# Difference operands kept in SBUF instead of streamed, with small tables fetched per stage

## The chip, the cores and the metric

The kernel runs on one core of a Trainium2 chip. The metric is the device time of one execution in microseconds (us). Three runs of the kernel before took 2766.94, 2767.81 and 2770.83 us; the median is 2767.81 us. A profile is one further execution, recorded by the hardware profiler. TensorE is called PE (its weight loads PEld), VectorE DVE, ScalarE ACT, GpSimd POOL and SyncE SP. SP and POOL are used here mainly to issue transfers, each from its own queue.

## The reference

A two-layer encoder works on 256 rows of 4096 numbers in float32. Cut to what matters:

```python
for l in range(DEPTH):                      # DEPTH = 2
    h = rmsnorm(x, norm_w[l])
    proj = h @ w_in[l]                      # 4096 -> 11264
    aq, ak, av, ag, rq, rk, rv, rg = jnp.split(proj, SPLIT_POINTS, axis=-1)
    aq = apply_axial_rope(rmsnorm(aq, q_norm[l]), rope) * attn_scale    # 16 heads
    ak = apply_axial_rope(rmsnorm(ak, k_norm[l]), rope)                 # 4 heads
    a_out = silu(ag) * gqa_attention(aq, ak, av)
    rq, rk = apply_axial_rope(rq, rope), apply_axial_rope(rk, rope) * ret_scale   # 8 heads
    r = bidirectional_retention(rq, rk, rv, log_gf, log_gb)             # decay by distance
    r_out = silu(rg) * rmsnorm(r, ret_norm[l])
    x = x + jnp.concatenate([a_out, r_out], axis=-1) @ w_out[l]         # 4096 -> 4096
return rmsnorm(x, final_norm)
```

Nearly all the arithmetic is in the two matrix products of each layer. The tables of cosines and sines, the distances between rows and the four norm weights are small.

## The kernel before, in words

**Products.** Every float32 product is made of three matmuls (`product`, lines 723 to 725): both factors are split into a high and a low part, and high times high, high times low and low times high are summed in PSUM. The operand, 256 rows of 4096 inputs, is kept in SBUF as 16 pairs of 256 inputs. The weights come from DRAM in pages of 128x1024 numbers (512 KB). A block computes two groups of 512 output columns from all 16 pairs. It saves multiplications with Strassen-like sums: the four pairs in `SEVEN` use seven products on sums of operand and weight quarters, the twelve others (`EIGHTS`) use eight products, two of which take a difference of the operand's two row halves. There are 11 blocks of the input projection and 4 of the output projection in a layer, 30 blocks in all, each with 372 matmuls of 512 columns. With 672 matmuls of 256 columns for attention and retention that makes 11832.

**Operand arrays.** `split_pair` makes a pair's arrays: `x7h`, `x7l` for the four, `x8h`, `x8l` for the twelve, and for each of the twelve also a difference array `x3` of 256 KB. The difference arrays do not stay in SBUF. They are stored to `x3_dram` (line 522, from a buffer called `xg`, or from the buffer of the first use where `direct` is set), and each block loads each of them again (`third`, line 1034) into one of `THIRDS` = 4 buffers. A load has to wait until PE has done with the pair that held the buffer before. In the profile the tile is called `x` and the DRAM array `x_dram`; `x2_dram`, the residual, has the same name there.

**Weights.** SP issues the page loads (line 366, tile `wraw`, 5 buffers). ACT rounds a page to its high part (`whi`), DVE subtracts to get the low part (`wlo`), and the buffer is then free for the next load. For the pairs in `SEVEN` DVE also makes sums of pages (`wsum`). One page in each group of four pairs is `far`: ACT makes its high part and the negative of it, and POOL issues a transfer that adds the page from DRAM to that (`flo`, line 391). That instruction is put in POOL's queue together with the two ACT instructions that it waits for.

**Order of the work.** The program is unrolled, and a planner that runs at build time sets the order on each engine: `Now` is its time, `ve` and `ac` add estimated durations of DVE and ACT work, and `LANDING` = 9 us is its estimate for a transfer. After each product `tick` puts in what there is time for: low parts, splits of the next operand, and steps of `tasks` (rotary, attention, retention and so on, of which only the first in the list is stepped) and `lanes`. `room` decides if there is time before the next weight page is due. Engines execute their instructions in that order, each waiting only for the semaphores it needs. If an estimate is too short, the waiting instruction holds up all that stands behind it on its engine.

**Pages.** Work arrays of 512 KB share `PAGES` = 10 buffers, counted in `held`. A new block takes two of them when its product M1 is done (`follow`, `combine`). If too many are held, or two heavy tasks are open, `follow` puts it off, and at the first of the last four products it runs tasks until there is room, whatever PE has to wait.

**Retention.** `retention_keys` stores rotated keys and queries to DRAM. `retention_weights` loads them for two heads (`rk`, `rq`, lines 886 and 887, from POOL), makes the decay array `D` out of the distances in `cst`, and multiplies by the scores that PE puts in the PSUM tile `ps`. `retention_pair` then multiplies by the values, norms, gates, transposes and puts the result away as operand for the output projection. The last two chunks of an operand (pairs 12 to 15) are not stored but split directly, late, during the first block that uses them.

**Small data.** The tables (`cst`, 512 KB), both layers' query and key norm weights (`qn`, `kn`) are loaded once by SP in `load_small` and stay in SBUF. A retention or final norm weight is loaded into a buffer `gain` of its own when it is needed.

Of the kernel before, what the change touches and what calls it, by code (L numbers as in the profile page):

```python
# [35 lines left out]
PAGES = 10  # L36
# [17 lines left out]

THIRDS = 4
# [150 lines left out]
def hybrid_encoder(  # L206
# [27 lines left out]
    x3_dram = tc.dram_tile([2, NP, P, 2, 2, P], F32R, name="x3_dram")  # L234
# [22 lines left out]
    cst = t(cp, [P, C_END], "cst")  # L257
    nw = t(cp, [P, DEPTH * KT], "nw")
    qn = t(cp, [P, DEPTH * HD], "qn")
    kn = t(cp, [P, DEPTH * HD], "kn")  # L260
# [9 lines left out]
    def load_small():  # L270
        nc.sync.dma_start(cst, consts)
        nc.sync.dma_start(dec, decay.partition_broadcast(P))
        nc.sync.dma_start(qn, q_norm.partition_broadcast(P))
        nc.sync.dma_start(kn, k_norm.partition_broadcast(P))

    def log_sigmoid():

        n = DEPTH * 2 * RET_HEADS
        u, s, s2, p, a = (t(cp, [P, n], f"ls{i}") for i in range(5))
# [13 lines left out]
        ve.tensor_scalar_mul(lgn, p, -2.0)  # L293

# [4 lines left out]
    def rope_tables(kind, l):  # L299

        cm = cst[:, C_COS:C_SIN].rearrange("p (m d) -> p m d", m=MT)
        sm = cst[:, C_SIN:C_D].rearrange("p (m d) -> p m d", m=MT)
# [4 lines left out]
        g = (kn if kind == "ak" else qn)[:, l * HD : (l + 1) * HD]  # L307
# [18 lines left out]
    class Weights:  # L326


        def __init__(self):
# [27 lines left out]
            self.raw, self.later = [], []  # L357
# [27 lines left out]
        def far_parts(self, g, src):  # L385

            g.hi = t(wp, [P, 2, NB], "fhi", FAR, F32R)
            g.lo = t(wp, [P, 2, NB], "flo", FAR, F32R)
            ac.copy(g.hi, src)
            ac.activation(g.lo, f32(g.hi), AF.Copy, scale=-1.0)  # L390
            nc.gpsimd.dma_start(g.lo, g.src[0], accum_op=ALU.add)  # L391
            g.high_at, g.low_at = ac.until, ac.until + FAR_LANDING
            self.load()

        def begin(self, g):
# [6 lines left out]
            elif g.kind == PAGE_A:  # L402
                self.a, self.b = self.raw.pop(0), self.raw.pop(0)
# [3 lines left out]
            elif g.kind == PAGE_T:  # L407
                self.u = t(wp, [P, 2, NB], "wsum", 2)
# [8 lines left out]

        def low_parts(self, all=False):
# [3 lines left out]
        def take(self):  # L422
            g = self.pages[self.at]
            self.at += 1
            while g.low_at is None:
                self.later.pop(0)[1]()
            return g

# [27 lines left out]
    stored_at = [0.0, 0.0]  # L456
    version = [0] * NP
    late, waiting, stored = [], [], set()

    def split_pair(p, v, l=None, direct=False):  # L460
# [22 lines left out]
        if p in SEVEN:  # L483
            hi = t(ap, [P, 7, P], "x7h", len(SEVEN), F32R)
# [14 lines left out]
            ve.tensor_sub(lo[:, 2:7, :], f, f32(hi)[:, 2:7, :])  # L499
        else:  # L500
            hi = t(ap, [P, 2, SEQ], "x8h", NP - len(SEVEN), F32R)
            lo = t(ap, [P, 2, SEQ], "x8l", NP - len(SEVEN), F32R)
            high(hi, v)
# [4 lines left out]
            if direct:  # L508
                while live[0] == THIRDS:
                    yield  # L510
                live[0] += 1
            else:
                while not stored_at:
                    yield
                free = stored_at.pop(0)
                if now.t < free:
                    yield free - now.t
            g = t(ap, [P, 2, 2, P], "x3" if direct else "xg", THIRDS if direct else 2, F32R)
# [3 lines left out]
            nc.gpsimd.dma_start(x3_dram[version[p] % 2, p], g)  # L522
            if direct:
                thirds[p] = g
            else:
                stored_at.append(ve.until + LANDING)
# [3 lines left out]
        operand[p] = (hi, lo)  # L530
# [3 lines left out]
    def split_operand(c, l=None, rest=0.0, direct=False):  # L534
        v, full[c] = full[c], None
        for k in range(2):
            p = 2 * c + k
            waiting.append(Lane(split_pair(p, v[:, 2 * k : 2 * k + 2, :], l, direct)))
            waiting[-1].pair, waiting[-1].ready = p, now.t + rest

    def split_late():
        split_operand(*late.pop(0), direct=True)
# [34 lines left out]
    class Turn:  # L577
# [19 lines left out]
        def step(self, forced=False):  # L597
# [6 lines left out]
            if c < self.fetched and self.freed > 2 * c + 1 and (forced or len(waiting) < SPLITS):  # L604
                split_operand(c, self.l, self.at[c] - now.t, self.first is not None)
# [28 lines left out]
    class Lane:  # L634
        def __init__(self, steps, heavy=True):
            self.heavy = heavy
            self.steps, self.ready, self.last, self.done, self.value = steps, 0.0, 0.0, False, None

        def step(self):
# [9 lines left out]
            if ac.until > a:  # L649
                self.last = max(self.last, ac.until)  # L650
            if rest == "PE":
# [8 lines left out]
    def clear():  # L660
        while tasks and tasks[0].done:
            tasks.pop(0)
        lanes[:] = [v for v in lanes if not v.done]

    def advance():

        clear()
        one = min(lanes + tasks[:1], key=lambda v: v.ready)
# [4 lines left out]
    def tick():  # L673

        weights.low_parts()
        while turning and turning[0].step():
            pass
        while True:
# [3 lines left out]
            for v in waiting[:SPLITS] + (lanes + tasks[:1] if room else []):  # L682
# [65 lines left out]
    def rotary(v, L, kind):  # L748
# [3 lines left out]
        C, S = L.tables.get(kind) or rope_tables(kind, L.index)  # L752
# [40 lines left out]
    def gate(acc, L, gain=None):  # L793
# [12 lines left out]
        if gain is not None:  # L806
            ve.tensor_mul(acc, acc, gain.unsqueeze(1).to_broadcast([P, MT, NB]))
        yield
# [73 lines left out]
    def retention_weights(L, i):  # L882
# [4 lines left out]
        nc.gpsimd.dma_start(qT, rq_dram[i])  # L887
        landed = max(now.t, L.stored) + LANDING
        D = page([P, 4, SEQ], "D")
        for e in range(2):  # L890
# [4 lines left out]
            ve.tensor_scalar_mul(v, cst[:, C_D:C_END], lf)  # L895
            ve.scalar_tensor_tensor(v, cst[:, C_D:C_END], lb, v, op0=ALU.mult, op1=ALU.min)
            yield
        ac.activation(D, D, AF.Exp)
# [53 lines left out]
    def retention_pair(L, i, gacc, vacc):  # L952
        gain = t(sp, [P, NB], "gain", 1)
# [7 lines left out]
        drop(4)  # L961
        mixT = gacc.rearrange("p m (a s) -> p (m a) s", a=2)
# [3 lines left out]
    def keys_values(L, kacc, vacc):  # L966
# [9 lines left out]
        L.tables = {}  # L976
        kT = yield from rotary(kacc, L, "ak")
# [410 lines left out]
```

## Time and profile before

| what | value |
|---|---|
| runs | 2766.94, 2767.81, 2770.83 us; median 2767.81 |
| profiled execution: time, span of its instructions | 2769.11 us, 2767.4 us |
| granted TensorE clock, mean | 0.987 |
| PE busy | 2646.9 us (96%) |
| DVE, ACT, POOL busy | 2067.6 (75%), 2024.1 (73%), 433.9 us (16%) |
| moved by transfers | 743.22 MB, mean 269 GB/s |
| SP's queue (q1), POOL's queue (q0), of the 16 engines' time | 54.1%, 31.2% |

A busy PE is not a PE that is never late: matmuls overlap, and a row lasts longer than the distance to the next one. What matters is that distance. In a stretch where nothing is late it is 0.227 us for 512 columns and 0.118 us for 256. The lines of the waits view give, for an engine and a line, who ended the idle time before it, in us in total, in times, and the longest. In the view by windows each row has the length of a stretch, then for each engine its busy time with the number of instructions, then the granted clock, the share of time in which the transfer engines were busy, and GB/s.

### The profile page before, as it was taken

The numbers are of one execution on the slowest core, as the hardware profiler recorded it, in microseconds if no ns is written. First come the engines' busy times: TensorE is split into PE (matmuls) and PEld (weight loads), VectorE is DVE, ScalarE is ACT, GpSimd is POOL, SyncE is SP. The second block draws the span as 40 slices with busy tenths as digits, with TensorE's granted clock in tenths as the row PEclk, the third lists the DMA queues.
The fourth block names the chain that finished last, engine by engine and source line by source line (L and its number), as shares of the span: only waits on it lengthen the run. The fifth ranks groups of instructions, "written<-read, shape, count | busy, mean of one in ns | idle before, by whom it ended". The sixth has DMA issues, their size and how long they took to land.

```text
span 2767.4 us, 35090 instructions
## 1 busy us (share of the span) xinstructions
PE 2646.9 (96%) x11832; PEld 2188.1 (79%) x11832; DVE 2067.6 (75%) x2489; ACT 2024.1 (73%) x3176; POOL 433.9 (16%) x665
## 2 busy tenths in 40 slices
PE   7999999999989999999899999999999899999997
PEld 5787788778878878888678877887888788788886
DVE  8786777778767887666678777777787588876665
ACT  6778888887657767666877688888876576775554
POOL 0121111111111121111121111111111112211110
PEclk9999999999999999999999999999999999999999
DMA  8997778778878998999898978887788799989996
GB/s 279 313 296 233 241 243 276 235 227 282 281 231 270 309 296 257 298 294 299 290 288 274 277 230 257 247 253 242 237 273 272 231 287 309 298 253 276 279 284 226
DMA packets 244724, 743.22 MB, mean 269 GB/s; under 512 B 26688, under 2 KB 33600, under 8 KB 244544
## 3 DMA queue, kind: packets, MB, share of 16 engines
q1 hardware_dynamic: 148048, 522.04, 54.1%
q0 software_dynamic: 96496, 218.93, 31.2%
q8 instruction: 94, 1.54, 0.2%
q14 instruction: 86, 0.70, 0.1%
HBM read 697.88 MB, written 42.99 MB: 268 GB/s over the span
## 4 chain that ended last, share of the span: by engine, by line
PE 68%; DMA 10%; DVE 9%; ACT 8%; issue 5%; POOL 1%; SPq 0%; DVEq 0%; ACTq 0%; POOLq 0%
PE M L724 22%; PE M L723 22%; PE M L725 22%; DMA wraw<-in_w_in 7%; DVE wlo L191 5%; ACT whi L191 2%; DMA rq<-rq_dram 2%; ACT pr L191 2%; PE ps L723 1%; PE ps L725 1%; PE ps L724 1%; ACT ca L191 1%; ACT rot L191 1%; DVE wsum L191 1%; ACT fhi L191 1%
## 5 line engine op out<-in xcount | busy, mean ns | idle before, releaser
L191 ACT CAST whi<-wraw 128x1024 fp32r<-128x1024 f32 x842 | 815.9, 988 | 463.8 <-PE M L725 283.1
L191 DVE TENSOR_TENSOR wlo<-wraw,whi 128x1024 fp32r<-128x1024 f32 x842 | 943.9, 1143 | 214.0 <-ACT whi L191 208.4
L724 PE MATMUL M<-wlo,x8h 128*128 128x512 f32 x1806 | 708.4, 392 | 5.6 <-DVE wlo L191 5.5
L723 PE MATMUL M<-whi,x8h 128*128 128x512 f32 x1806 | 707.8, 392 | 4.5 <-ACT whi L191 4.5
L725 PE MATMUL M<-whi,x8l 128*128 128x512 f32 x1806 | 706.3, 391 | 0.0
L724 PEld LDWEIGHTS M<-wlo,x8h 128*128 128x128 f32 x1806 | 341.8, 189 | 77.8 <-DVE wlo L191 8.2
L723 PEld LDWEIGHTS M<-whi,x8h 128*128 128x128 f32 x1806 | 342.0, 189 | 75.4 <-ACT whi L191 4.9
L725 PEld LDWEIGHTS M<-whi,x8l 128*128 128x128 f32 x1806 | 341.8, 189 | 71.6
L191 DVE TENSOR_TENSOR wlo<-wsum,whi 128x1024 fp32r<-128x1024 f32 x240 | 292.7, 1220 | 86.0 <-ACT whi L191 85.5
L724 PE MATMUL M<-wlo,x7h 128*128 128x512 f32 x840 | 329.3, 392 | 13.5 <-DVE wlo L191 13.5
L725 PE MATMUL M<-whi,x7l 128*128 128x512 f32 x840 | 328.1, 391 | 6.5 <-DVE x7l L191 6.5
L723 PE MATMUL M<-whi,x7h 128*128 128x512 f32 x840 | 328.4, 391 | 4.2 <-DVE cb L191 4.1
L1034 POOL DMA_DIRECT2D x<-x_dram x339 | 227.7, 717 | 663.7 <-PE M L725 636.7
L191 ACT CAST whi<-wsum 128x1024 fp32r<-128x1024 f32 x240 | 251.8, 1049 | 97.4 <-PE M L725 92.9
L191 DVE TENSOR_TENSOR wsum<-wraw 128x1024 f32<-128x1024 f32 x120 | 146.7, 1222 | 192.9 <-DMA wraw<-in_w_in 111.7
L724 PE MATMUL M<-wlo,x 128*128 128x512 f32 x602 | 236.7, 393 | 14.8 <-DVE wlo L191 14.8
L723 PE MATMUL M<-whi,x 128*128 128x512 f32 x602 | 236.0, 392 | 11.6 <-ACT whi L191 11.6
L725 PE MATMUL M<-whi,x 128*128 128x512 f32 x602 | 235.5, 391 | 0.0
L391 POOL DMA_DIRECT2D flo<-in_w_in x86 | 76.1, 885 | 855.6 <-ACT flo L191 788.2
L724 PEld LDWEIGHTS M<-wlo,x7h 128*128 128x128 f32 x840 | 158.4, 189 | 49.6 <-DVE wlo L191 17.8
L725 PEld LDWEIGHTS M<-whi,x7l 128*128 128x128 f32 x840 | 158.5, 189 | 39.9 <-DVE x7l L191 7.2
L723 PEld LDWEIGHTS M<-whi,x7h 128*128 128x128 f32 x840 | 158.4, 189 | 38.2 <-DVE cb L191 4.9
(222 smaller groups left out, 3511.8 us busy)
## 6 DMA issues: line engine op xcount, KB each, us to landing
wraw<-in_w_in SPq DMA_DIRECT2D x703, 512.0 KB, 5.1
wraw<-in_w_out SPq DMA_DIRECT2D x256, 512.0 KB, 5.8
x<-x_dram POOLq DMA_DIRECT2D x339, 256.0 KB, 7.4
flo<-in_w_in POOLq DMA_DIRECT2D x86, 512.0 KB, 7.5
flo<-in_w_out POOLq DMA_DIRECT2D x32, 512.0 KB, 7.7
full<-next_dram POOLq DMA_DIRECT2D x18, 512.0 KB, 9.7
next_dram<-ca POOLq DMA_DIRECT2D x15, 512.0 KB, 7.6
x_dram<-xg POOLq DMA_DIRECT2D x27, 256.0 KB, 6.0
```

The lines of the kernel that those rows point to most:

```text
L191: return call(out, *args, **kwargs)
L391: nc.gpsimd.dma_start(g.lo, g.src[0], accum_op=ALU.add)
L723: nc.tensor.matmul(out, a[0], b[0], start=start, stop=False)
L724: nc.tensor.matmul(out, a[0], b[1], start=False, stop=False)
L725: nc.tensor.matmul(out, a[1], b[0], start=False, stop=stop)
L1034: nc.gpsimd.dma_start(thirds[p], x3_dram[(phase - 1) % 2, p])
```

## The change

`x3_dram`, `third` and `THIRDS` go. Each of the twelve difference arrays has a buffer of its own in SBUF, is written once for each operand by `split_pair`, and is read there by every block. The split no longer waits for a free buffer or a finished store. To make room, `cst`, `qn`, `kn`, the buffer `gain` and the arrays of `log_sigmoid` go, and there are 9 pages instead of 10. A stage fetches what it needs into a shared page: `plain_tables` loads cosines and sines, and for attention the two norm weights, when `keys_values` or `retention_keys` begins; `retention_weights` loads the distances as `dist`; a norm weight takes a page as well.

Three rules of the planner change too. The transfer that completes a far page is put into POOL's queue when ACT's part is planned to be done (`adds`), and not with it. Only one pair of `SEVEN` at a time is in the middle of its split (`sums_of`), and low parts of an older sum of pages are put in before a new sum is made (`sums_low`). A retention pair that has only its transpose left counts as `tail`: the next retention weights may then be stepped beside it, and it no longer holds off the next block.

```diff
-PAGES = 10
+PAGES = 9
-THIRDS = 4
...
-    cst = t(cp, [P, C_END], "cst")
-    qn = t(cp, [P, DEPTH * HD], "qn")
-    kn = t(cp, [P, DEPTH * HD], "kn")
...
+    def plain_tables(l=None):
+        v = page([P, 3, SEQ], "tables")
+        nc.sync.dma_start(v[:, :2, :], consts[:, C_COS:C_D].rearrange("p (a b) -> p a b", a=2))
+        if l is not None:
+            for i, g in enumerate((k_norm, q_norm)):
+                nc.sync.dma_start(
+                    v[:, 2, i * HD : (i + 1) * HD], g[l * HD : (l + 1) * HD].partition_broadcast(P)
+                )
+        return v
...
-            nc.gpsimd.dma_start(g.lo, g.src[0], accum_op=ALU.add)
             g.high_at, g.low_at = ac.until, ac.until + FAR_LANDING
+            self.adds.append((ac.until, partial(nc.gpsimd.dma_start, g.lo, g.src[0], accum_op=ALU.add)))
...
+        def add(self, now_all=False):
+            while self.adds and (now_all or self.adds[0][0] <= now.t + 0.5):
+                self.adds.pop(0)[1]()
...
+            g = t(ap, [P, 2, 2, P], "x3", NP - len(SEVEN), F32R)
             high(hi, v)
             yield
             low(lo, v, hi)
             ve.tensor_sub(x0, x0, x1)
             yield
-            if direct:
-                while live[0] == THIRDS:
-                    yield
-                live[0] += 1
-            else:
-                while not stored_at:
-                    yield
-                free = stored_at.pop(0)
-                if now.t < free:
-                    yield free - now.t
-            g = t(ap, [P, 2, 2, P], "x3" if direct else "xg", THIRDS if direct else 2, F32R)
             high(g[:, 0], x0)
             yield
             low(g[:, 1], x0, g[:, 0])
-            nc.gpsimd.dma_start(x3_dram[version[p] % 2, p], g)
-            if direct:
-                thirds[p] = g
-            else:
-                stored_at.append(ve.until + LANDING)
...
+    def running():
+        return tasks[: 2 if len(tasks) > 1 and tasks[0].tail and not tasks[1].heavy else 1]
...
         nc.gpsimd.dma_start(qT, rq_dram[i])
+        dist = page([P, 2 * SEQ], "dist")
+        nc.sync.dma_start(dist, consts[:, C_D:C_END])
+        yield LANDING
...
-            ve.tensor_scalar_mul(v, cst[:, C_D:C_END], lf)
-            ve.scalar_tensor_tensor(v, cst[:, C_D:C_END], lb, v, op0=ALU.mult, op1=ALU.min)
+            ve.tensor_scalar_mul(v, dist, lf)
+            ve.scalar_tensor_tensor(v, dist, lb, v, op0=ALU.mult, op1=ALU.min)
...
-        gain = t(sp, [P, NB], "gain", 1)
+        gain = page([P, NB], "gain")
...
+        yield "tail"
         mixT = gacc.rearrange("p m (a s) -> p (m a) s", a=2)
...
         L.tables = {}
+        L.plain = plain_tables(L.index)
         kT = yield from rotary(kacc, L, "ak")
...
     def retention_keys(L, r, kacc, qacc):
+        L.plain = plain_tables()
+        yield LANDING
...
-            if finished[0][0] == "M1" and (held[0] > PAGES - 2 or sum(v.heavy for v in tasks) > 1):
+            if finished[0][0] == "M1" and (held[0] > PAGES - 2 or sum(v.heavy and not v.tail for v in tasks) > 1):
...
-    def third(p, phase):
-        need(p, phase)
-        if p in thirds:
-            return
-        live[0] += 1
-        thirds[p] = t(ap, [P, 2, 2, P], "x3", THIRDS, F32R)
-        nc.gpsimd.dma_start(thirds[p], x3_dram[(phase - 1) % 2, p])
...
-                a = [x3[p][:, i, index[0], :] for i in range(2)]
+                a = [operand[p][2][:, i, index[0], :] for i in range(2)]
```

## The prediction

> **What bounds the kernel now.** I read the page first, then the stretches by window, then who PE waited for, then single stalls in the timeline. The page and the view of transfers give the engines, the two queues and the traffic that the change removes:
>
> ```profile
> span 2767.4 us, 35090 instructions
> PE 2646.9 (96%) x11832; PEld 2188.1 (79%) x11832; DVE 2067.6 (75%) x2489; ACT 2024.1 (73%) x3176; POOL 433.9 (16%) x665
> ...
> q1 hardware_dynamic: 148048, 522.04, 54.1%
> q0 software_dynamic: 96496, 218.93, 31.2%
> ...
> x<-x_dram POOLq DMA_DIRECT2D x339, 256.0 KB, 7.4
> ...
> x_dram<-xg POOLq DMA_DIRECT2D x27, 256.0 KB, 6.0
> x_dram<-x POOLq DMA_DIRECT2D x21, 256.0 KB, 5.6
> ```
>
> PE is the bound, but not by 96%. In fed stretches the timeline starts a 512-column matmul every 0.2268 us (49.07, 49.30) and a 256-column one every 0.118 (797.66, 797.78). 11160 x 0.2268 + 672 x 0.118 = 2610 us that no schedule here takes away. PE starts at 9.7 us, its last matmul at 2750.7; what follows, 16.6 us, is the end. The rest, 2767.4 - 9.7 - 2610.2 - 16.6 = 131 us, is lost on the way. The window view shows where; each line is a length, then PE's busy time:
>
> ```profile
> 389.00:477.00 88.00, 88.00 (x407) 73.54 (x406) 68.80 (x77) 76.52 (x133) 14.88 (x22) 1.00 0.86 268
> 755.00:856.00 101.00, 91.27 (x412) 75.92 (x411) 66.81 (x74) 64.19 (x94) 14.42 (x22) 0.95 0.76 232
> 940.00:1038.00 98.00, 92.38 (x423) 76.82 (x422) 85.96 (x125) 68.13 (x105) 21.90 (x36) 0.98 0.92 299
> 1287.00:1386.00 99.00, 89.88 (x377) 72.06 (x377) 68.75 (x100) 71.97 (x126) 20.97 (x34) 0.95 0.90 288
> 1386.00:1480.00 94.00, 88.25 (x371) 71.40 (x370) 72.89 (x103) 69.62 (x113) 16.10 (x25) 0.96 0.91 280
> ```
>
> A quiet block loses nothing, even with transfers busy 86% of the time. The others lose 6 to 12 us, partly at a lower granted clock. I split the trace by blocks of 372 large matmuls and took each one's length less its 0.2268 and 0.118 steps. The first block loses 17.9, attention blocks (2 to 6 and 17 to 21) 44.3, block 1 1.8, retention blocks (7 to 10, 22 to 25) 43, and blocks 14 and 15, where layer 1 begins, 24.0. PE's waits name the causes:
>
> ```profile
> PE M L724 <- DVE wlo L191: 33.9, 21, 3.0
> PE ps L723 <- DMA rq<-rq_dram: 29.2, 4, 9.7
> PE M L723 <- ACT whi L191: 16.1, 4, 9.7
> PE M L725 <- DVE x7l L191: 6.5, 2, 5.0
> ```
>
> The last fence shows two kinds of them, one at 777 to 792 us, one at 339 to 353: POOL's issues, PE's stall, and what DVE waited for.
>
> ```profile
> 777.80 0.88 POOL L887 DMA_DIRECT2D rq<-rq_dram  x1
> 792.29 0.58 PE L723 MATMUL ps<-rq,rk 128*128 128x256 f32 x1 [9.73 <-DMA rq<-rq_dram]
> 339.24 0.88 POOL L391 DMA_DIRECT2D flo<-in_w_in  x1 [11.61 <-ACT flo L191]
> 339.80 0.88 POOL L1034 DMA_DIRECT2D x<-x_dram  x1
> 341.60 0.54 POOL L1034 DMA_DIRECT2D x<-x_dram  x1 [0.92 <-PE M L725]
> 349.76 0.53 POOL L1034 DMA_DIRECT2D x<-x_dram  x1 [7.62 <-PE M L725]
> 352.58 1.23 DVE L191 TENSOR_TENSOR wsum<-wraw 128x1024 f32<-128x1024 f32 x1 [4.17 <-DMA wraw<-in_w_in]
> ```
>
> **The change part by part.** Of the built programs I take only order: a distance between two instructions is counted in the matmuls between them, at 0.2268 us. Arithmetic is untouched: PE, DVE and ACT have the same instructions. POOL issues 244 transfers instead of 631 (339 loads and 48 stores of 256 KB less, 101 MB of 743); SP issues 1036 instead of 1021.
>
> *Retention loads, -36 us.* Before, the scores stand 13 and 26 large matmuls (2.9 and 5.9 us) behind the issue of `rq` in the second and fourth retention pair of a layer: the planner was forced, since a new block could not begin while two heavy tasks were open. Such a load lands in 6.7 to 14.4 us, so PE stood 9.9, 5.4, 9.3 and 5.2 us, and restarted at half speed. Blocks 8, 10, 23 and 25 lose 38.2 us in all. Afterwards, through `tail`, the scores stand 76 to 91 matmuls (17 to 21 us) behind it. I leave 2 us. The delay of retention by 80 to 150 matmuls that buys this lies under weight products; it costs at the end of each layer (below).
>
> *Retention scores, -4.* The waits of 2.4 and 2.0 us in blocks 7 and 22 (loss 4.9) sit behind a page that took 10.7 us. The two scores move from 15 to 48 matmuls apart.
>
> *Late weight pages in attention, -15; at 107 us, -2.* Nine DVE stalls end with a page (as at 352.58), and PE waits 18.0 us behind them, some 20 with slow restarts. POOL's queue explains them: `flo` holds it until ACT is done, then `flo` and two or three `x` loads go out together. At 344.9 to 352.5 us 2.75 MB were in flight, 0.75 of it `x`. If landing follows the bytes, 7.6 us becomes 5.5, more than the 1.6 us that PE waited. The same sum leaves 1.8 of 3.2 at 213 us, 0.7 of 2.3 at 332, and nothing to 0.8 at the others: 4.5 stay. At 107 us 0.75 of 4.75 MB go: 1.7 off. If landing did not depend on `x`, this item is 0; if every such stall goes, -22.
>
> A different split is thinkable. The Trainium skill, DMA: Bandwidth & Descriptors, section Queues, rings and completion order, states that each transfer engine takes turns between queues, a packet of each. By that, a page is slowed as long as POOL's queue holds anything at all, and `flo`, `kv` and stores stay there; bursts would only end sooner, and this item and the next would be nearer the small end. The trace of before cannot tell: every late page of attention had `x` beside it.
>
> *Start of layer 1, -14.* Blocks 14 and 15 lose 24.0 us. At 1296 us 6.25 MB are in flight, 0.75 of it `x`; `ca<-in_x` takes 15.5 us where the planner counts 9. POOL stood 11.3 us for a store, with other stores behind it. In the new order the residual's stores come up to 75 matmuls (17 us) earlier and the last splits up to 28 (6 us). I take a little over half; bounds -6 and -22, since the chain of store, load and split remains.
>
> *The burst at 114 us, -2.* Block 1 loses 1.75 us behind the steps of `log_sigmoid`; they now stand apart.
>
> *Tables for the keys, +5.* New, and with no time given to land: in block 1 the table products stand 10 matmuls (2.3 us) behind SP's issue of the key norm, with a low part behind them that PE needs 13 matmuls after that issue. The nearest transfer is `gain`, 3.7 to 12.5, median 4.6 us; `kn` took 8.9. With 4.6, DVE goes on 20 matmuls after the issue, spends 0.95 us on the tables (143.25 to 144.20) and 1.2 on the low part: PE waits 3.7 us, and about 1 more at half speed. Ends: 2.8 at 3.7 and 8.0 at 8.9; I take the median, being of the same size and form. In layer 1 the next low part has 5 us of slack: 0 at 4.6, 3.3 at 8.9. I take 0.5.
>
> *Distances, +1; norm weights, 0.* Eight `dist` loads (256 KB) have 7.0 to 8.2 us before DVE reads them; 3 of 14 `gain` loads took over 9. Bounds 0 and +8. `gain` has 6.1 to 10.4 us, before 5.2 to 9.1, and nobody waited for it then. The rotary tables have 9.1 to 10.7.
>
> *Late splits, +3.* Pairs 14 and 15 of each mixer output come later: the array that PE first needs is written 3 matmuls before its use, against 40 before. I put 1.5 us each, between 0 and the 5.2 us of the other late operand (45.81 us). Nine pages instead of ten cause no forced work elsewhere in the order.
>
> *Unchanged:* the start to 47 us (the same order, 15.4 us lost, DVE full), four stalls in each layer's attention behind ACT's queue (`room` waiting for `pr`), 17 us in all, the 16.6 us at the end. `flo` has 13.9 us or more until its use, and lands in 7.6 (11.7 at most).
>
> Sum: -36 - 4 - 15 - 2 - 14 - 2 + 5 + 0.5 + 1 + 3 = -63.5. The profiled execution took 2769.1 us, 1.3 above the median, so it stands for the runs; 2767.8 - 63.5 = **2704** us.
>
> **The rivals.**
>
> *Small relief.* Pages land no sooner. For it: a stretch at 96% transfer share (1480 to 1565 us) loses nothing, one at 76% (198 to 295) does, so share is not what counts, and `flo` and `kv` remain in the bursts. Then only the order helps: -36 - 1 - 6 - 2, and +7 and +3 for tables, +2 for distances, +3 for late splits: -30, 2738 us. Against it: every late page of attention had `x` beside it.
>
> *Larger relief.* Shorter bursts also clear the start of layer 1 and all late pages: -38 - 5 - 22 - 2 - 22 - 2 + 3 + 1 = -87, 2681 us. Against it: the chain from residual to split has transfers of its own.
>
> *Slower: SP's fetches hold DVE.* DVE runs in order, and a table that is late holds low parts that PE needs. 22 fetches a run are exposed. They have 2.3 to 10.7 us, 8.2 on average; to eat 63.5 us they must be 2.9 us late on average, so land in 11.1. At 11.5 us the time would be 22 x 3.3 - 63.5 = +9, 2777 us. Against it: 1 of 14 `gain` loads took that long.
>
> *The arrays are fetched all the same.* Excluded: no load of `x3` is left in the order.
>
> **How the numbers follow.** Forecast 0.62, small relief 0.19, larger relief 0.08, slower 0.09, within 0.2% (5.5 us, about what a measurement here can tell) 0.02. The range, 2676 to 2742, leaves out slower and part of the small relief. Faster 0.89.
>
> **What would show it.** `x<-x_dram` gone from the transfer lines, 640 MB instead of 743; no PE wait for `rq`; in PE's waits `wlo` from 34 to about 20; a PE stall of 3 to 6 us near 120 to 150 us behind a DVE wait for `tables`; a page's median landing from 5.4 to below 5; blocks 14 and 15 at 10 us lost. I am wrong if DVE or PE waits for `dist`, `tables` or `gain` add up to tens of us, if SP's queue waits on a page buffer, or if late pages wait as long as now.

## The result, and the profile after

The changed kernel takes 2701.78 us (median of four runs, 2699.30 to 2705.79), the kernel before 2767.38 us in the same comparison: a ratio of 0.9769, 95% interval 0.9744 to 0.9793. The profiled execution took 2701.46 us with a span of 2699.7 us. PE's first matmul starts at 11.1 us, the last at 2682.9; with the same 2610 us of steps, 61.7 us are lost on the way, against 130.9 before.

The page of the changed kernel gives the span and the engines (busy time, share, number of instructions):

```profile
span 2699.7 us, 34139 instructions
...
PE 2633.3 (98%) x11832; PEld 2182.0 (81%) x11832; DVE 2068.9 (77%) x2489; ACT 2025.1 (75%) x3176; POOL 218.1 (8%) x278
```

Its view of transfers gives the traffic, the two queues, and for a kind of transfer the number, the size and the median time to landing:

```profile
DMA packets 191149, 644.82 MB, mean 239 GB/s; under 512 B 20736, under 2 KB 27904, under 8 KB 190976
...
q1 hardware_dynamic: 150208, 525.19, 56.4%
q0 software_dynamic: 40768, 117.46, 19.9%
...
wraw<-in_w_in SPq DMA_DIRECT2D x703, 512.0 KB, 4.5
wraw<-in_w_out SPq DMA_DIRECT2D x256, 512.0 KB, 4.8
```

The difference arrays are gone from POOL's queue (218.93 MB there before), DVE and ACT do what they did, and a weight page lands sooner (medians 5.1 and 5.8 us before). The view by windows, cut at the blocks that answer to the five shown of before (4, 8, 10, 14, 15), gives for each stretch the length, PE's busy time, and near the end the granted clock and the share of transfer time:

```profile
386.00:475.00 89.00, 89.00 (x411) 74.35 (x411) 69.44 (x78) 77.50 (x135) 6.97 (x8) 1.00 0.76 232
745.00:837.00 92.00, 92.00 (x438) 77.38 (x438) 73.66 (x86) 63.95 (x93) 8.85 (x11) 1.00 0.76 233
921.00:1011.00 90.00, 89.03 (x411) 74.09 (x409) 82.17 (x117) 62.97 (x90) 13.68 (x20) 1.00 0.87 283
1269.00:1359.00 90.00, 86.14 (x371) 70.13 (x370) 70.96 (x104) 73.23 (x129) 10.41 (x14) 0.98 0.83 270
1359.00:1445.00 86.00, 85.51 (x377) 70.16 (x376) 71.27 (x99) 67.92 (x111) 7.80 (x9) 1.00 0.84 252
```

The blocks of the two retention stretches had lost 11.9 and 7.7 us at a clock of 0.95 and 0.98; now they lose 0.2 and 1.3 us and the clock is 1.00. The start of layer 1 shrinks from 99 and 94 us to 90 and 86. PE's waits name what is left (us in total, times, longest):

```profile
PE M L735 <- DVE wlo L189: 26.7, 15, 5.0
PE M L734 <- ACT whi L189: 11.6, 2, 11.1
PE M L736 <- DVE x7l L189: 6.0, 2, 5.0
```

No line for `rq` remains; 29.2 us stood there before. What is new stands in block 1, where the timeline shows DVE's last work before the tables, SP's fetch of the key norm, DVE's first use of the tables with the idle time before it, the low part behind it, and PE:

```profile
137.02 1.82 DVE L189 TENSOR_TENSOR wlo<-wraw,whi 128x512 fp32r<-128x512 f32 x2
...
140.16 0.66 SPq L298 DMA_DIRECT2D tables<-in_k_norm  x1
...
146.39 0.29 DVE L189 TENSOR_TENSOR C<-tables 128x128 f32<-128x128 f32 x1 [7.55 <-DMA tables<-in_k_norm]
147.34 1.22 DVE L189 TENSOR_TENSOR wlo<-wsum,whi 128x1024 fp32r<-128x1024 f32 x1
148.61 0.79 PE L735 MATMUL M<-wlo,x7h 128*128 128x512 f32 x1 [5.05 <-DVE wlo L189]
```

So the time is near the forecast of 2704 us, and the blocks that gained are those that it named. The question for the experiments is whether they gained for the reasons given.

### The profile page after: what moved, and what is told of

Its sections match the earlier page's. It is cut to its first block, busy times and chain, and to the rows that moved or that the text cites. A ratio compares the mean times of both kernels' runs of the same rounds, so it can differ in the third digit from the quotient of the medians.

```text
span 2699.7 us, 34139 instructions
## 1 busy us (share of the span) xinstructions
PE 2633.3 (98%) x11832; PEld 2182.0 (81%) x11832; DVE 2068.9 (77%) x2489; ACT 2025.1 (75%) x3176; POOL 218.1 (8%) x278
## 4 chain that ended last, share of the span: by engine, by line
PE 79%; DVE 7%; ACT 5%; issue 4%; DMA 4%; SPq 0%; POOL 0%; DVEq 0%; POOLq 0%; ACTq 0%
PE M L735 26%; PE M L734 25%; PE M L736 25%; DVE wlo L189 4%; DMA wraw<-in_w_in 3%; ACT pr L189 2%; ACT whi L189 2%; DMA wraw<-in_w_out 1%; PE ps L736 1%; PE ps L734 1%; PE ps L735 1%; DVE ca L189 0%; DVE cb L189 0%; DVE wsum L189 0%; ACT fhi L189 0%
## 5 line engine op out<-in xcount | busy, mean ns | idle before, releaser
L189 ACT CAST fhi<-wraw 128x1024 fp32r<-128x1024 f32 x118 | 124.2, 1052 | 73.6 <-PE M L736 64.8
```

What stands on the lines that cost most here:

```text
L189: return call(out, *args, **kwargs)
```

## The experiments

The table holds every kernel: the median time, the ratio to before with its interval, and PE's loss in groups of blocks in the profiled run (the length of a block less its 0.2268 and 0.118 steps, as in the prediction). *Attention* is blocks 2 to 6 and 17 to 21, *retention* 8, 10, 23 and 25.

| kernel | us | ratio | block 1 | attention | retention | 11, 26 | 14, 15 |
|---|---|---|---|---|---|---|---|
| before | 2767.4 | 1 | 1.8 | 44.3 | 38.2 | 0.1 | 24.0 |
| changed | 2701.8 | 0.9769 (0.9744 to 0.9793) | 7.2 | 28.3 | 2.6 | 0.3 | 7.4 |
| changed, no `tail` | 2736.8 | 0.9906 (0.9883 to 0.9930) | 7.7 | 26.7 | 2.9 | 34.9 | 7.4 |
| before + `tail` | 2733.4 | 0.9874 (0.9850 to 0.9899) | 1.0 | 46.2 | 5.3 | 0.1 | 21.3 |
| before + wait | 2744.3 | 0.9916 (0.9894 to 0.9938) | 0.5 | 47.0 | 7.8 | 4.3 | 22.2 |
| before + `adds` | 2725.3 | 0.9864 (0.9837 to 0.9891) | 1.9 | 36.7 | 7.4 | 0.1 | 16.9 |
| changed, streamed | 2743.9 | 0.9924 (0.9896 to 0.9952) | 10.8 | 45.3 | 6.0 | 11.9 | 21.6 |
| changed, half streamed | 2718.2 | 0.9821 (0.9798 to 0.9844) | 7.4 | 32.5 | 3.6 | 6.7 | 13.4 |
| changed, `adds` undone | 2706.4 | 0.9790 (0.9763 to 0.9818) | 7.3 | 27.2 | 2.5 | 0.3 | 14.4 |
| changed, tables early | 2691.6 | 0.9743 (0.9722 to 0.9764) | 0.0 | 28.9 | 2.5 | 0.2 | 7.1 |
| and softmax put off | 2677.4 | 0.9678 (0.9658 to 0.9698) | 0.0 | 9.8 | 3.8 | 0.3 | 6.8 |

Block 0 and the start of the first matmul (8.4 to 11.1 us) scatter by a few us between runs of all kernels and are left out.

### Is it `tail` that keeps rq ahead of its scores?

The prediction's largest term, the retention loads, rests on `tail`. The first kernel takes it out of the changed one.

```diff
         drop(4)
-        yield "tail"
         mixT = gacc.rearrange("p m (a s) -> p (m a) s", a=2)
```

> The changed kernel without the rule that a retention pair with only its transpose left counts as tail; all else is as changed. Theory A (the prediction's step on the retention loads): tail is what keeps rq ahead of its scores, so PE's waits for rq come back (some 25 to 30 us, four of them, in the second and fourth pair of a layer) and the time is 30 to 36 us above the changed kernel, 2732 to 2738 us. Theory B: the loads are early because the new wait for the distances stands ahead of the moment from which the landing of rq is counted (about 18 us of allowance, 9 before) and because POOL's queue is shorter; tail only lets the end of a layer's retention keep up. In the order of this kernel the scores stand 79, 84, 78 and 111 large matmuls behind the issue of rq, which speaks for B. Then no wait for rq above 1 us; the loss comes in blocks 11 and 26, where the split of pairs 14 and 15 is late, by about 13 us in each: about 2728 us. The times are near each other; the row of rq and the loss of blocks 8, 10, 11, 23, 25 and 26 tell the two apart.

It took 2736.8 us: inside theory A's interval by its time. The rows say the opposite. These are PE's waits in the kernel without `tail`, the longest three, and no line for `rq` follows:

```profile
PE M L734 <- ACT x L189: 29.1, 2, 14.6
PE M L735 <- DVE wlo L189: 26.9, 13, 5.1
PE M L734 <- ACT whi L189: 11.1, 2, 10.3
```

The retention blocks lose 2.9 us as in the changed kernel. The loss stands in blocks 11 and 26, 17 us each, where PE waits 14.6 us for a split of pair 14 or 15 (`x` is the difference array of such a pair) and restarts at half speed. In the changed kernel `rq` does not need `tail`; what `tail` does there is to let a layer's retention end in time for the late splits. Theory B holds, with its price sized at 13 instead of 17 us a layer.

Then what makes `rq` late before? Each of the three rules that touch it was put alone into the kernel before. First `tail`:

```diff
+        return tasks[: 2 if len(tasks) > 1 and tasks[0].tail and not tasks[1].heavy else 1]
...
+        yield "tail"
...
-            if finished[0][0] == "M1" and (held[0] > PAGES - 2 or sum(v.heavy for v in tasks) > 1):
+            if finished[0][0] == "M1" and (held[0] > PAGES - 2 or sum(v.heavy and not v.tail for v in tasks) > 1):
```

> The kernel before with the tail rule alone (a retention pair with only its transpose left lets the next retention weights step beside it and no longer holds off a block). The difference arrays are streamed, the distances stay in SBUF, and no wait is added. In the built order the scores stand 73, 62, 87 and 42 large matmuls behind the issue of rq (before: 73, 13, 87, 26), that is 16.6, 14.1, 19.7 and 9.5 us; such a load landed in 6.7 to 14.4 us before. If tail alone is enough (the prediction's mechanism), PE's waits for rq shrink from 29.2 us to under 3 and blocks 8, 10, 23 and 25 lose under 10 us instead of 38: 2730 to 2738 us. If the load is late because of POOL's queue and slow landing whatever tail does, rq waits of 10 us or more stay: 2745 us or more.

The time is 2733.4 us, and of 29.2 us this is left in PE's waits:

```profile
PE ps L728 <- DMA rq<-rq_dram: 1.6, 2, 0.8
```

So `tail` alone is enough where nothing else is changed, though it isn't needed where the rest is. Next the wait that the change adds for the distances, in the kernel before, where the distances don't need it:

```diff
         nc.gpsimd.dma_start(qT, rq_dram[i])
+        yield LANDING
         landed = max(now.t, L.stored) + LANDING
```

> The kernel before with one line more: the wait of LANDING (9 us of planned time) that the change puts into retention_weights, behind the issue of rk and rq and ahead of the moment from which their landing is counted. No tail, difference arrays streamed, distances in SBUF. In the built order the scores stand 79, 58, 93 and 94 matmuls behind the issue of rq: 17.9, 13.2, 21.1 and 21.3 us. If the allowance alone is enough (theory B), PE's waits for rq go from 29.2 us to under 3; the retention of a layer ends later without tail, so that blocks 11 and 26 may lose up to 10 us each in late splits (17 each in the changed kernel without tail): 2733 to 2753 us. If only tail or the shorter queue cures it, rq waits of 10 us or more stay and the time is 2755 us or more.

2744.3 us. No wait for `rq` is left among PE's waits; the retention blocks lose 7.8 instead of 38.2 us and blocks 11 and 26 lose 4.3. The added 9 us of allowance are enough too. What both work around is seen in POOL's timeline of the kernel before, ahead of the issue of `rq` at 777.80 us that the prediction shows:

```profile
763.82 0.54 POOL L1034 DMA_DIRECT2D x<-x_dram  x1 [9.44 <-PE M L725]
775.65 0.88 POOL L391 DMA_DIRECT2D flo<-in_w_in  x1 [11.30 <-ACT flo L191]
776.22 0.87 POOL L1034 DMA_DIRECT2D x<-x_dram  x1
776.75 0.88 POOL L572 DMA_DIRECT2D next_dram<-ca  x1
777.27 0.88 POOL L886 DMA_DIRECT2D rk<-rk_dram  x1
...
1006.20 0.54 POOL L522 DMA_DIRECT2D x_dram<-xg  x1 [7.01 <-issue]
1009.08 0.88 POOL L391 DMA_DIRECT2D flo<-in_w_in  x1 [2.34 <-ACT flo L191]
```

In the second pair POOL stands 11.3 us at the transfer that completes a far page, until ACT is done with it. Four more transfers stand behind it, `rq` the last of them, and go out within 2.2 us: `rk` lands in 12.4, `rq` in 14.4 us. In the fourth pair (the last two lines) POOL is idle 7.0 us before the store of a difference array and 2.3 us before a far page; `rq` goes out at 1010.76 us and lands in 11.0. Layer 1 repeats both, at 2150.78 and 2382.65 us.

The planner had left its 9 us for `rq`. Its own order, as it comes out when the kernel before is built, has 42 large matmuls (9.5 us) between the issue and the scores in both pairs, and no block was put off until it had to force a step. In the built program, which lists the engines' queues together, 13 and 26 are left, since POOL's queue is behind there too. With `tail` alone the planner still leaves 42 in the second pair, and the built program has 62: the issue stands elsewhere in POOL's queue, where POOL waits 5.3 us at the far page ahead of it. The third rule of the change, `adds`, is aimed at the far page, and the prediction gave it no term. It changes nothing that the planner counts, and yet moves the built distances to 33 and 37. Alone in the kernel before:

```diff
-            nc.gpsimd.dma_start(g.lo, g.src[0], accum_op=ALU.add)
             g.high_at, g.low_at = ac.until, ac.until + FAR_LANDING
+            self.adds.append((ac.until, partial(nc.gpsimd.dma_start, g.lo, g.src[0], accum_op=ALU.add)))
...
+            if g.far:
+                self.add(True)
...
+        weights.add()
```

> The kernel before with one rule of the change alone: the transfer that completes a far page is put into POOL's queue when ACT's part is planned to be done, and not with it. In the profile of before POOL stands 11.3 us at such a transfer until 775.65 us, with the store of an operand and the loads of rk and rq behind it; then five transfers go out within 2.2 us. In the built order of this kernel the scores stand 73, 33, 91 and 37 large matmuls behind the issue of rq (before: 73, 13, 87, 26), so 7.5 and 8.4 us in the second and fourth pair instead of 2.9 and 5.9. If POOL's blocked queue is what makes rq late, about half of PE's 29.2 us for rq goes (4.6 and 2.5 us less in each layer, 14 us in all, more if the transfers no longer go out in one burst): 10 to 16 us stay and blocks 8, 10, 23 and 25 lose 18 to 26 us instead of 38: about 2745 to 2755 us. If the lateness has nothing to do with that queue, the waits stay above 24 us and the time within 5 us of 2765.

It gave more than was expected: 2725.3 us, below the 2745 to 2755, with 4.6 us of waits for `rq`. The waits of this kernel, PE's for `rq`, then POOL's for PE at a load of a difference array and for ACT at a far page:

```profile
PE ps L730 <- DMA rq<-rq_dram: 4.6, 2, 2.9
...
POOL x L1041 <- PE M L732: 1300.4, 218, 13.3
POOL flo L433 <- ACT flo L191: 330.5, 93, 18.0
```

POOL's two lines of before:

```profile
POOL flo L391 <- ACT flo L191: 1081.5, 102, 18.0
POOL x L1034 <- PE M L725: 636.7, 114, 18.5
```

POOL waits hardly less in all: what it no longer waits at far pages it waits at the loads of `x`, whose buffer PE still holds. What changed is what stands behind the waiting instruction. In the second pair of layer 0 `rq` lands in 10.7 instead of 14.4 us; the median landing of `x` falls from 7.4 to 5.9 us, that of `rq` from 9.4 to 7.5. The faster landing is why the waits for `rq` shrink by more than the shift in order. Attention and the start of layer 1 gain too (7.6 and 7.1 us). A weight page's median is no better than before there (5.3 and 5.8 us), but DVE's waits for pages before a sum fall from 192.8 to 150.6 us; that fewer bursts make the worst pages less late is the likely reason, and not shown page by page. One rule of a few lines, with the arrays still streamed, gives 1.4% of the whole change's 2.3%.

### Do the bytes of the difference arrays make pages late?

The changed kernel with the arrays streamed again, and everything else kept:

```diff
-            g = t(ap, [P, 2, 2, P], "x3", NP - len(SEVEN), F32R)
+            g = t(ap, [P, 2, 2, P], "x3" if direct else "xg", THIRDS if direct else 2, F32R)
...
+            nc.gpsimd.dma_start(x3_dram[version[p] % 2, p], g)
...
+        nc.gpsimd.dma_start(thirds[p], x3_dram[(phase - 1) % 2, p])
```

> The changed kernel with the difference arrays streamed from DRAM again (48 stores and 339 loads of 256 KB on POOL's queue); the shared pages, the tables per stage, tail, the put-off transfer of far pages and the rules for sums stay. If the traffic and its place in POOL's queue made the gains in attention and at the start of layer 1 (the prediction: 15 and 14 us, measured 16 and 17), blocks 2 to 6 and 17 to 21 lose 40 us or more instead of 28, blocks 14 and 15 lose 20 or more instead of 7, a page's median landing goes back from 4.6 to about 5.4 us, and the time is 2725 to 2745 us. If the new order and the put-off far transfers made them, these blocks stay within 4 us and the time is at most 2708 us. PE's waits for rq: the scores stand 76 to 86 matmuls behind the issue here too, so both expect none.

2743.9 us, as the traffic theory had it. Attention loses 45.3 us again and the start of layer 1 21.6. The landing of a page goes back, and past the 5.1 and 5.8 us of before, in the view of transfers of this kernel:

```profile
wraw<-in_w_in SPq DMA_DIRECT2D x703, 512.0 KB, 5.4
wraw<-in_w_out SPq DMA_DIRECT2D x256, 512.0 KB, 6.2
x<-x_dram POOLq DMA_DIRECT2D x339, 256.0 KB, 5.9
```

Retention stays cured (waits for `rq` of 0.8 us). Something not expected came in blocks 11 and 26, 11.9 us. Two of the four waits in this line, 3.5 us each, stand there; why DVE's sums (`cb`) are late at that place was not followed further:

```profile
PE M L753 <- DVE cb L191: 11.1, 4, 3.5
```

Streaming brings bytes, but also 387 more instructions in POOL's queue, many of which wait for PE or DVE. To part the two, the low half of each array was streamed and the high half kept: the same transfers at the same places, of half the size. Against the streamed kernel:

```diff
-            g = t(ap, [P, 2, 2, P], "x3" if direct else "xg", THIRDS if direct else 2, F32R)
-            high(g[:, 0], x0)
+            gh = t(ap, [P, 2, P], "x3h", NP - len(SEVEN), F32R)
+            g = t(ap, [P, 2, P], "x3" if direct else "xg", THIRDS if direct else 2, F32R)
+            high(gh, x0)
             yield
-            low(g[:, 1], x0, g[:, 0])
+            low(g, x0, gh)
```

> The changed kernel with the difference arrays streamed again, but by halves: the high part of each stays in SBUF, the low part is stored and loaded. The number of transfers, their place in POOL's queue and the waits of that queue are those of the fully streamed kernel (2743.9 us); the bytes are half (387 transfers of 128 KB). If the bytes in flight make pages late, the loss that streaming brought in attention (45.3 us against 28.2), blocks 14 and 15 (21.6 against 7.4) and 11 and 26 (11.9 against 0.3) falls by about half, the median landing of a page lies between 4.6 and 5.4 us, and the time is 2716 to 2728 us. If the number of transfers and the waits in POOL's queue make them late, the time stays within 6 us of 2744.

2718.2 us: of the 42.1 us that full streaming costs, 16.4 remain at half the bytes, and a page lands in between.

```profile
wraw<-in_w_in SPq DMA_DIRECT2D x703, 512.0 KB, 4.8
wraw<-in_w_out SPq DMA_DIRECT2D x256, 512.0 KB, 5.7
x<-x_dram POOLq DMA_DIRECT2D x339, 128.0 KB, 5.1
```

So most of the loss goes with the bytes: had the number of transfers or the waits of the queue made it, the time would have stayed near 2744 us. What share those have in the 16.4 us that remain is not told apart. The groups don't halve alike: attention keeps 4.2 of 17.1 us, the start of layer 1 6.0 of 14.2, blocks 11 and 26 6.4 of 11.5. A page that lands before it is needed costs nothing, which would explain why in all the first half of the bytes was worth more than the second.

The rule `adds`, worth so much before, was then taken out of the changed kernel.

```diff
-            self.adds.append((ac.until, partial(nc.gpsimd.dma_start, g.lo, g.src[0], accum_op=ALU.add)))
+            nc.gpsimd.dma_start(g.lo, g.src[0], accum_op=ALU.add)
```

> The changed kernel, with the transfer that completes a far page put into POOL's queue at once with ACT's two instructions, as before the change. POOL then stands until ACT is done with the page, with whatever was issued later behind it. If the queue was blocked mostly to the harm of the loads of the difference arrays, which are gone, this is worth little: within 4 us of the changed kernel, 2698 to 2706 us. If the blocked queue itself was what made rq, kv and the pages late, waits for rq or late pages come back: 10 to 25 us more, 2712 to 2727 us.

2706.4 us, 4.6 more than the changed kernel's median and so just past the 4 us that were expected at most, with intervals of the ratio that overlap (0.9763 to 0.9818 against 0.9744 to 0.9793). Retention and attention lose nothing by it. Only blocks 14 and 15 lose 7.0 us more, in one profiled run. With few transfers left behind it, the blocked queue harms almost nobody: in the changed kernel itself POOL waits 1538.0 us for ACT at far pages, more than in the kernel before, and no `rq` is late. The sum of a queue's waits is no measure of their harm.

### The tables, and a better version

The fetch for attention's keys, moved ahead of the values' step of its stage:

```diff
     def keys_values(L, kacc, vacc):
+        L.plain = plain_tables(L.index)
         v = yield from values(vacc, L)
...
         L.tables = {}
-        L.plain = plain_tables(L.index)
         kT = yield from rotary(kacc, L, "ak")
```

> The changed kernel, with the fetch of the tables and norm weights for attention's keys moved ahead of the values' step in the same stage; SP issues it 7.0 us before DVE's first table product in block 1, where it has 2.3 us now (2.5 us in layer 1). If the two DVE waits for these tables (13.1 us in total) are what block 1 loses, PE's stall of 5.2 us at 148.6 us shrinks to 0 to 1 us and block 1 goes from 7.2 us lost to about 2: 2696 to 2698 us. If something else held PE there (the low parts themselves are too many), block 1 stays above 5 and the time within 2 us of 2701.8.

2691.6 us, below the 2696 to 2698 that were expected, and block 1 loses nothing. Of DVE's two waits for these tables (13.1 us) this one is left, in layer 1, where no PE stall follows it:

```profile
DVE C L189 <- DMA tables<-in_k_norm: 4.7, 1, 4.7
```

That is 10.2 us in the median for a block that had lost 7.2: the rest is more than this move explains in the profile (the first matmul came 1.8 us earlier, which scatters), and stays open.

The stalls that remained in attention, counted in the prediction as unchanged, sit behind DVE instructions that wait for ACT's softmax scaling. One more line lets the planner do other work in between:

```diff
                 ac.activation(w, w, AF.Copy, scale=st[:, 1, 2 * e + m : 2 * e + m + 1])
         rows_done.append(h)
+        yield
         room = page([P, MT, NB], "room")
```

> The changed kernel with the tables early (2691.6 us) and one more line: after the four scalings of the softmax in attention_pair the planner may do other work before it orders DVE's transpose of their result. Now the transpose is put into DVE's queue while ACT has several us of work ahead of its input; DVE stood 55.4 us in 14 such waits (up to 7.1), with low parts behind it, and PE stalled 17 us at them. If that order is the cause, DVE's waits for these scalings fall below 20 us, the four stalls of 1 to 3 us in each layer's attention go, and the time is 2676 to 2682 us. If the time that ACT needs is itself the limit, the stalls move to the transposed softmax (pTl) and the time stays within 3 us of 2691.6.

2677.4 us, ratio 0.9678 (0.9658 to 0.9698): faster than both kernels. In the changed kernel's timeline DVE stood 5 us at such a transpose, with low parts behind it:

```profile
274.75 0.17 DVE L189 RECIPROCAL st<-st 128x4 f32<-128x4 f32 x1
279.93 1.25 DVE L189 STREAM_TRANSPOSE room<-pr 128x1024 f32<-128x1024 f32 x1 [5.00 <-ACT pr L189]
281.09 1.18 DVE L189 TENSOR_TENSOR wlo<-wraw,whi 128x1024 fp32r<-128x1024 f32 x1
```

With the line added, two low parts stand between the reciprocal and the transpose:

```profile
263.20 0.18 DVE L189 RECIPROCAL st<-st 128x4 f32<-128x4 f32 x1 [3.62 <-ACT pr L189]
264.13 1.23 DVE L189 TENSOR_TENSOR wlo<-wraw,whi 128x1024 fp32r<-128x1024 f32 x1 [0.76 <-ACT whi L189]
266.45 0.69 DVE L189 TENSOR_TENSOR wlo<-wraw,whi 128x512 fp32r<-128x512 f32 x1 [1.09 <-ACT whi L189]
268.06 1.25 DVE L189 STREAM_TRANSPOSE room<-pr 128x1024 f32<-128x1024 f32 x1 [0.92 <-ACT pr L189]
```

DVE's waits of this kind fall from 55.4 to 18.2 us, and attention loses 9.8 us where it had lost 28.9 with the tables early:

```profile
DVE room L189 <- ACT pr L189: 18.2, 8, 4.2
```

One kernel has no time: the changed one with the landing of `rq` counted from its issue, without the 9 us that the distances add. In that order engines wait for one another without end, so whether the shorter queue alone would keep `rq` ahead there, with `tail`, is not shown.

## Why the prediction was right, and where it was not

The time, 2702 against 2704 us, and the range held. By the terms of its sum (measured by blocks, in one profiled run of each):

- *Retention loads, -36.* Measured -35.6, by **the wrong cause**. The step that failed is "the planner was forced, since a new block could not begin while two heavy tasks were open", with its sequel "Afterwards, through `tail`, the scores stand 76 to 91 matmuls (17 to 21 us) behind it". The distances in the built program were right, the reason was not: no step was forced, the planner had left 42 matmuls, and without `tail` the changed kernel has 78 to 111 and no wait for `rq`. `rq` was late because POOL stood 11.3 us at `flo` (in the fourth pair 7.0 at a store and 2.3 at `flo`) and then let what had gathered go at once. In the kernel before `tail`, the added wait and `adds` each bring the waits for `rq` from 29.2 to under 5 us, and the change has all three; that the term came out at its size says nothing for its reason. The rows were there: the prediction read POOL's queue at 339 us, but not ahead of 777 us.
- *Tail's price, late splits, +3.* Measured +0.2. Here the prediction saw `tail` as a cost; it is the reverse, for without it these blocks lose 34.9 us.
- *Retention scores, -4.* Measured -3.4.
- *Late pages in attention, -15, and at 107 us, -2.* Measured -16.1 and -2.8 (block 0 scatters by more than that). Right in mechanism: streaming the arrays again costs these blocks 17.1 us, half the bytes 4.2. The sum left out that `adds` alone would have given 7.6 of it.
- *Start of layer 1, -14.* Measured -16.6. Both causes count: streaming costs 14.2 there, `adds` undone 7.0. The second, again, is not in the prediction, which named the bytes and the order of the stores.
- *The burst and the tables in block 1, -2 and +5.* Measured together +5.4. The mechanism was as told, from SP's fetch through DVE's order to PE. The two sizes were off and made up for each other in part, which is luck: the key norm was there 6.2 us after its issue and not 4.6, so that PE stood 5.2 us instead of 3.7, and the restart cost 2 us and not 1 (below).
- *Tables in layer 1, +0.5; distances, +1.* Nothing in block 16. Of eight fetches of the distances one made DVE wait, 1.5 us, and no PE stall was traced to it.

Of the rivals, *small relief* would have had attention keep its late pages, *larger relief* would have cleared the start of layer 1 (7.4 us are still lost there), and *slower* asked for fetches that land in 11 us; the one wait of 7.5 us for tables is the nearest that came to it. Four of the six signs that the prediction named came out as told: `x<-x_dram` gone at 645 MB, no `rq`, a page's landing at 4.5 to 4.8 us, a PE stall in block 1. `wlo` fell to 26.7 instead of 20 us, 5.0 of which are that stall, and blocks 14 and 15 lost 7.4 instead of 10.

The measured terms come to -68.9 us, where the sum had -63.5. The fit of the total says little about the reason for its largest term. Three rules each give it or nearly, and the prediction saw one of them, by a wrong reading of what made `rq` late. For a change that held everything but `tail`, the same reasoning would have put the waits for `rq` back, which don't come, and would have missed the 35 us in blocks 11 and 26, which do.

## What to carry to other kernels

When a load lands late, look ahead of its issue in the queue that issued it: an instruction there that waits for another engine delays all that is behind it, and then releases it in one burst, in which each transfer was slow as well (`rq` 14.4 us here, 4.9 in the same pair of the changed kernel); putting such an instruction into the queue only when its input is due gave 1.4% here by itself. When several rules of a change could have brought a gain, test each alone and each left out, and read the rows and not the time: without `tail` the time was the one that the wrong theory asked for. On an engine that works in order, an instruction that is put in as soon as it can be named, and not when its input is ready, is a wait for everything behind it; one point at which the planner may order other work was worth 14 us.

## What the runs showed of the hardware

**A page's landing follows what the other queue holds.** For each page load I counted what SP and POOL had issued and not landed when it was issued (512 KB for a page, `flo` and what else is not a small load, 256 KB for `x`; an estimate by issues, not by packets). With one other page ahead in SP's queue, the median landing was:

| on POOL's queue | before | changed |
|---|---|---|
| nothing | 3.7 us (200 pages) | 3.6 us (280) |
| 0.25 to 0.5 MB | 3.7 us (71) | 5.0 us (95) |
| 0.75 to 1 MB | 5.7 us (80) | 6.1 us (21) |
| 1.25 MB or more | 7.3 us (45) | 7.2 us (15) |

Of some 960 pages 410 met 0.75 MB or more before, 122 after. The prediction weighed a rule of the Trainium skill against this (DMA: Bandwidth & Descriptors, section Queues, rings and completion order: each transfer engine takes turns between the queues that have work, a packet of each), and drew from it that a page is slowed as long as POOL's queue holds anything at all. What it drew from that for its sum, attention and the start of layer 1 nearer the small end, did not come: they gained 16.1 and 16.6 us, the landing grows with what POOL's queue holds, and half the streamed bytes at the same places cost 16.4 instead of 42.1 us. The table does not speak against the turns themselves: with two queues taking turns a page would land in up to about twice its 3.7 us (an estimate), as in the last row. Whether they are as the page says, no run here shows.

**A restart at half pace costs about 2 us, and 3 us of stall are near the edge.** A stall is counted here as the distance between the starts of two matmuls less the usual 0.227 us. After the stall of 5.2 us at 148.61 us the next matmuls start 0.59, eight times 0.427 and 0.25 us apart, then 0.227: 2.0 us more than at full pace. After 3.0 us of stall (282.33) it was one of 0.59, six of 0.427 and one of 0.36, 1.7 us; after the two of 14.7 us in the kernel without `tail` 3.0 and 2.1 us. But the stalls of the same 3.0 us at 282.12 and 1651.33 us in the kernel before were followed by full pace. In the eleven traces together, half pace followed 26 of 47 stalls of 2.0 to 2.7 us, 19 of 24 of about 3.0, and all 32 above 3.15, where it cost 1.5 to 3.0 us. The Trainium skill (TensorE: Matmul & The Clock Gate, section What's actually happening) gives half the clock after an idle window of about 3.4 us and full clock after as long a busy one; the trace agrees on the length (eight steps of 0.427 make 3.4 us at half pace after the stall of 5.2), and shows half pace after shorter stalls as well. A PE stall of more than 3 us is to be counted here with some 2 us on top, one of 2 to 3 us with the chance of it.

**Small fetches were not fast behind pages.** The two fetches of a key norm, 64 KB spread to all partitions, landed in 6.1 and 7.1 us and the 256 KB of tables in 7.0 in the median, while a page of 512 KB took 4.5 and `gain`, 256 KB spread in the same way, 5.2 for retention and 6.3 for the final norm. In block 1 SP had issued three pages in the 3.4 us before the tables; how much of the 6.1 us is the wait behind them was not tested. A small load is no reason to leave less time for it.
